# x loaded by features alone, its squares summed by TensorE, and a new order for the first stage of a diffusion block

## The chip, the cores and the metric

One core of one Trainium2 chip runs the whole kernel. The metric is device time in microseconds. One execution was also profiled; every time in the tables below is from that execution, unless it is called a median of the runs.

## What is computed

The reference is one layer of a hybrid block over 1024 tokens (a grid of 16 rows and 64 columns) of 1024 features, with 256 context tokens. Cut to what matters:

```python
def hybrid_layer(x, ctx, c, c_ctx, w_ada, b_ada, norm_g, w_in, ...):
    shift, scale, gate = adaln(c, w_ada, b_ada)           # silu(c) @ w_ada + b_ada
    shift_c, scale_c, gate_c = adaln(c_ctx, w_ada, b_ada)
    h = rmsnorm(x, norm_g) * (1 + scale) + shift          # mean of squares over the features
    hc = rmsnorm(ctx, norm_g) * (1 + scale_c) + shift_c
    q, k, v, za, u, bg, cg, zc = split(h @ w_in)          # 8 x 512 columns
    ...
    attn = neighbourhood_attention(q, k, v, kc, vc, rpb) * silu(za)
    conv = bg * conv3(cg * u) * silu(zc)
    return x + gate * (concat([attn, conv]) @ w_out)
```

All inputs and the output are float32.

## The kernel before, in words

Tokens lie in four blocks of 256. A float32 matrix product is made as three products of parts: each operand is split into a high part, rounded to the type that TensorE takes at full pace, and a low part, the rest (`hh` and `hl` for the normed x, `w[:, 0]` and `w[:, 1]` for a weight chunk). A step `fc` of one letter of these three is three products, one for each of three groups of 128 weight columns.

The stages follow one another: the first one (to about 64 us) makes the modulation, the normed x and the first three column groups; then come the q, k, v projections (the `pacc` products), attention with the gate projections as filler (`pu`), and the output product (`pout`).

The first stage is what the change touches. It is written as a list of words, `LOADS` and `STEPS` (lines 36 to 49), which `do` (line 750) reads one after the other; each word calls one helper through the table `does` (line 732). A number behind a word is a feature tile, k, of 128 features, or half and feature tile, or half, feature tile and which of the three products. While `strict` holds the engines (line 553), each engine and SyncE, which issues the loads, runs its instructions in exactly the order of the words. So an instruction that waits holds all that stand behind it on its engine. The words:

- `x`, `n`: rows of x or of the context, 128 tokens by 1024 features, 512 KB. `t` (half, k): x by features, 128 features by 512 tokens, 256 KB. `s` k: a slab of modulation weights, 1 MB, three buffers. `c` k, `q` k: a weight chunk of 128 by 384, 192 KB, five buffers, for the first column groups and for the first `pacc` tile. `e`: the context by features. `g`: gain tables.
- `sq` (line 584): ScalarE squares a row tile and sums it over the features by its accumulator. `root`: VectorE adds epsilon, GpSimd takes the power -1/2. `Rt` and `R` (line 595): TensorE spreads the 512 factors over all partitions, ScalarE copies them to SBUF.
- `T` (line 633): TensorE turns the first two feature tiles of half 0 out of the rows; `v` (line 637) multiplies these by the factors.
- `pr` (line 603): the modulation products of one slab, 32 narrow products. `tp`, `ab` (lines 611, 615): VectorE turns them and makes scale and shift of feature tile k.
- `u`, `hi`, `lo` (lines 623, 649, 655): VectorE scales a feature tile, ScalarE adds the shift and rounds to the high part, VectorE makes the low part. Scaling and low part are one VectorE instruction each, with both tensors in SBUF.
- `ch`, `cl` and `qh`, `ql` (lines 673, 678): a chunk's high part by ScalarE, its rest by VectorE. `rg` (line 699): VectorE multiplies rotation tables by gains, GpSimd prepares the gains.
- `fc` (line 665): the products of a feature tile with its chunk; product 0 is high by high, 1 takes the chunk's rest, 2 takes the low part of x.
- `warm`, `fill`: products of zeros that fill TensorE's waits. `conv`: steps of the gated convolution on the finished groups.

Behind the stage, line 1188 starts the first `pacc` tile (`proj_tile`, line 307), which reads the chunks' high parts and rests in the order of k. Much later, the loop over attention quarters (line 1321, n to 34) and line 1449 lead into the last stage; ScalarE's function there changes from Exp to Silu at the gates `zs` (line 500), which loads a table.

## Time and profile before

| | us |
|---|---|
| median of 3 runs | 590.03 (589.93 to 590.26) |
| profiled execution, its own time | 589.67 |
| its span | 587.8 |
| TensorE busy | 578.4 |
| VectorE busy | 438.9 |
| ScalarE busy | 282.2 |
| GpSimd busy | 57.4 |
| first `acc` product starts | 16.58 |
| first `pacc` product starts | 63.83 |

A profile row reads: start, duration, engine, line, operation, output <- inputs, shapes, count, and in brackets the idle time of the engine just before it and what ended that. PE is TensorE, DVE VectorE, ACT ScalarE, POOL GpSimd, SP SyncE. All instructions that go through the ordering helper carry line 71, so rows are told apart by their tiles. In a row of windows, the numbers behind each engine are its busy time and its count, then come the clock that TensorE was granted, the share of the DMA engines and GB/s. In a row of waits stand the total, the number of waits and the longest.

### The profile page before, as it was taken

Reading aid. Unit: us, or ns where it says so; the run is one execution under the profiler, and the core shown is the slowest. Engines: PE = TensorE matmul, PEld = TensorE weight load, DVE = VectorE, ACT = ScalarE, POOL = GpSimd, SP = SyncE. Lnnn points to the kernel's source line nnn. Section 1 sums busy time; section 2 is a strip of 40 time slices with the busy share of each in tenths; the row PEclk is TensorE's granted clock in tenths of the full one; section 3 lists DMA queues with packets and bytes.
Section 4 is the critical chain, followed back from the end, with each engine's and each line's share of the span. In section 5 each row is a group of like instructions: output and inputs, shape, how many; then the busy total and the mean of one; then the engine's idle time right before and its main releaser. Section 6 shows DMA issues by size and latency. Waiting matters only on the chain.

```text
span 587.8 us, 9905 instructions
## 1 busy us (share of the span) xinstructions
PE 578.4 (98%) x3532; PEld 483.4 (82%) x3532; DVE 438.9 (75%) x890; ACT 282.2 (48%) x652; POOL 57.4 (10%) x82
## 2 busy tenths in 40 slices
PE   8899999999999999999999999999999999999997
PEld 4578899999999999988878787878787866888886
DVE  1578779755846745367998788998978897999952
ACT  5636355436525546333463464466545646543420
POOL 1001024123123222100000000000000001100000
PEclk9999999999999999999999999999999999999999
DMA  8997576946765786685253647555757273673532
GB/s 327 410 413 268 177 258 188 308 149 219 247 207 186 249 302 233 213 314 200 92 191 129 241 139 224 195 209 160 251 188 254 93 251 114 231 249 88 200 125 90
DMA packets 66678, 126.14 MB, mean 215 GB/s; under 512 B 8713, under 2 KB 27649, under 8 KB 64324
## 3 DMA queue, kind: packets, MB, share of 16 engines
q1 hardware_dynamic: 66244, 124.70, 60.9%
q0 software_dynamic: 384, 0.81, 0.6%
q8 instruction: 28, 0.46, 0.3%
q14 instruction: 22, 0.18, 0.1%
HBM read 92.38 MB, written 33.10 MB: 213 GB/s over the span
## 4 chain that ended last, share of the span: by engine, by line
PE 89%; DMA 4%; DVE 3%; ACT 2%; issue 1%; SPq 0%; POOL 0%; DVEq 0%; ACTq 0%
PE pu L71 29%; PE pacc L71 22%; PE pout L71 13%; PE acc L71 5%; PE po L71 4%; PE cacc L71 4%; PE pss L71 3%; DMA xn<-in_xb 3%; PE pc L71 3%; PE pmx L71 2%; PE trA L71 1%; PE tr L71 1%; DMA y_d<-tb 1%; PE trB L71 1%; ACT sqj L71 1%
## 5 line engine op out<-in xcount | busy, mean ns | idle before, releaser
L71 PE MATMUL pu<-h,uh 128*128 128x512 f32 x544 | 174.6, 402 | 0.5 <-ACT zs L71 0.5
L71 PE MATMUL pacc<-w,h 128*128 128x384 f32 x768 | 138.9, 337 | 1.1 <-ACT ub L71 0.6
L71 PEld LDWEIGHTS pacc<-w,h 128*128 128x128 f32 x768 | 132.7, 188 | 1.9 <-ACT ub L71 1.1
L71 PEld LDWEIGHTS pu<-h,uh 128*128 128x128 f32 x544 | 97.3, 188 | 19.3 <-issue 1.2
L71 PE MATMUL pu<-h,ul 128*128 128x512 f32 x272 | 106.5, 392 | 0.0
L71 PE MATMUL pout<-right,left 128*128 128x512 f32 (+2 forms) x348 | 77.0, 383 | 0.0
L71 PEld LDWEIGHTS pout<-right,left 128*128 128x128 f32 x348 | 64.4, 188 | 12.7
L71 PEld LDWEIGHTS pu<-h,ul 128*128 128x128 f32 x272 | 51.1, 188 | 11.5
L71 POOL TENSOR_TENSOR ss<-ss,few 128x4 f32<-128x4 f32 (+1 forms) x40 | 41.4, 1035 | 126.7 <-DVE ss L71 126.4
L71 ACT COPY sc<-pc 128x512 f32<-128x512 f32 x32 | 18.7, 587 | 44.8 <-PE pc L71 44.8
L71 ACT ACTIVATE sc<-sc 128x512 f32<-128x512 f32 x32 | 20.3, 633 | 34.3 <-DVE sc L71 34.1
L71 PE MATMUL acc<-h,w 128*128 128x512 f32 x144 | 35.3, 397 | 1.4 <-ACT h L71 1.4
L71 ACT ACTIVATE sq<-pacc 128x256 f32<-128x256 f32 x32 | 12.4, 387 | 47.0 <-PE pacc L71 46.3
L71 DVE TENSOR_TENSOR sum<-sum,sb 128x372 f32<-128x372 f32 (+2 forms) x64 | 31.1, 486 | 2.8
L71 DVE SCALAR_TENSOR_TENSOR m<-pout,ab,m 128x512 f32<-128x512 f32 (+2 forms) x34 | 22.9, 717 | 13.2 <-PE pout L71 13.1
L71 PEld LDWEIGHTS acc<-h,w 128*128 128x128 f32 x144 | 26.3, 188 | 7.8 <-ACT h L71 2.1
L71 ACT ACTIVATE qn<-pacc,ss 128x64 f32<-128x64 f32 x128 | 30.0, 330 | 4.9 <-PE trA L71 2.5
L71 DVE TENSOR_TENSOR mx<-mx,sb 128x372 f32<-128x372 f32 (+2 forms) x64 | 30.8, 482 | 1.4
L71 DVE TENSOR_REDUCE ss<-sq 128x4 f32<-128x260 f32 (+1 forms) x40 | 15.7, 393 | 21.6 <-ACT sq L71 21.5
L71 DVE TENSOR_TENSOR ul<-uraw,uh 128x512 fp32r<-128x512 f32 x34 | 23.1, 686 | 9.4 <-ACT uh L71 9.4
L71 DVE TENSOR_TENSOR sb<-pss,bt 128x192 f32<-128x192 f32 (+3 forms) x48 | 27.6, 602 | 2.5 <-PE pss L71 2.5
L71 DVE TENSOR_TENSOR sb<-sb,mg 128x744 f32<-128x744 f32 (+2 forms) x32 | 26.6, 833 | 0.0
(142 smaller groups left out, 848.6 us busy)
## 6 DMA issues: line engine op xcount, KB each, us to landing
uraw<-in_w_col SPq DMA_DIRECT2D x34, 256.0 KB, 4.2
slab<-in_w_mod SPq DMA_DIRECT2D x8, 1024.0 KB, 8.9
q_d<-qs SPq DMA_DIRECT2D x32, 256.0 KB, 4.3
k_s<-k_d SPq DMA_DIRECT2D x8, 1024.0 KB, 7.3
q_s<-q_d SPq DMA_DIRECT2D x16, 512.0 KB, 3.7
wr<-in_w_grp SPq DMA_DIRECT2D x40, 192.0 KB, 5.0
bt<-in_rpb SPq DMA_DIRECT2D x8, 564.0 KB, 7.2
xn<-in_xb SPq DMA_DIRECT2D x8, 512.0 KB
```

Source lines behind the costliest of these rows:

```text
L71: i = emit(*a, **kw)
```

## The change

x is no longer loaded by rows. All 16 tiles by features are loaded, those of half 0 first, into the place that later holds feature tiles 6 and 7 of the normed x. The sums of squares are made from them: ScalarE squares the even and VectorE the odd feature tiles (`xs`), TensorE multiplies each by ones, in four groups of 128 tokens, which add up over the features in one bank (`xp`), ScalarE copies the bank (`cp`), TensorE turns the four rows into columns (`sl`), VectorE adds epsilon out of that bank (`root`, now `shifted`), and GpSimd takes the power as a word of its own (`po`). The first scaled tile reads the spread factors from PSUM.

All rests of chunks but the first, and the gain tables, are made by GpSimd and not by VectorE. The shift of a feature tile is made by ScalarE (`sh`). The small vectors come turned from the host, so TensorE and VectorE no longer turn them. The order of all words is new: half 1 follows half 0 by several feature tiles, the three products of a tile need not come together, and `done` counts them to mark the first and last of a bank. An activation of Silu on one element is put behind the last attention quarter.

```diff
-LOADS = "x0 x1 x2 x3 s0 c0 s1 c1 x4 x5 x6 x7 t10 t11 s2 t02 t12 c2"
+LOADS = "t00 t01 t02 t03 i0 t04 t05 t06 t07 s0 c0 s1 c1 s2 c2"
 STEPS = [
...
+    "ch7 rg0 u12 fc061 hi11 tp7 qh0 lo06 fc101 sh7 ab7 hi12 lo11 u07 u13 qh2 fc060 fc100 hi13 lo12 u14 fc102",
...
-    vec = bmp.tile([P, 3 * 384], F32, name="vec", tag="bt", bufs=2)[:, :P]
-    sp.dma_start(vec[:nvec], vecs)
-    sp.dma_start(ci, cst[:, 0:P])
+    sp.dma_start(vecT, vecs)
...
+    def feature_square(half, k):
+
+        squares[half, k] = xp.tile([P, 512], F32, name="sqf", tag="sqf", bufs=3)
+        if k % 2:
+            dve.scalar_tensor_tensor(squares[half, k], xh[half, k], 1.0 / D, xh[half, k], ALU.mult, ALU.mult)
+        else:
+            act.activation(squares[half, k], xh[half, k], AF.Square, scale=1.0 / 32)
+
+    def stat_bank(half):
+        return acc0[2 * half][1]
+
+    def feature_sum(half, k):
+
+        v = squares.pop((half, k))
+        for g in range(4):
+            pe.matmul(stat_bank(half)[32 * g:32 * g + 32, :P], onef, v[:, g * P:(g + 1) * P],
+                      start=taken[half] == 0, stop=taken[half] == KT - 1, skip_group_check=True)
+        taken[half] += 1
+
+    def sums_copy(half):
+        tokens[half] = xp.tile([P, P], F32, name="tk", tag="tk", bufs=1)
+        act.copy(tokens[half], stat_bank(half)[:, :P])
+
+    def sums_turned(half):
+        pe.matmul(stat_bank(half)[:, 256:260], tokens[half], ident[:, 0:P:32], start=True, stop=True)
...
-        dve.tensor_scalar(a[:, 0], rows[k][:, 0:2], bsh[:, k:k + 1], None, ALU.add)
+
+    def shift(k):
+        a = ab[:, k].rearrange("p (w j) -> p j w", w=2)
+        act.activation(a[:, 0], rows[k][:, 0:2], AF.Identity, bias=bsh[:, k:k + 1])
...
-        dve.tensor_tensor(v, early(k), spread_r[0], ALU.mult)
+        dve.tensor_tensor(v, xh[0, k], turns[0] if k == 0 else spread_r[0], ALU.mult)
...
-        dve.tensor_tensor(w[:, 1], raw, w[:, 0].bitcast(F32), ALU.subtract)
+        (dve if raws is chunks and k == 0 else pool).tensor_tensor(w[:, 1], raw, w[:, 0].bitcast(F32), ALU.subtract)
...
-        dve.tensor_tensor(tables[1][:, n, :, k], rraw, gqk[:, k:k + 1].broadcast_to([P, NB, HD]), ALU.mult)
+        pool.tensor_tensor(tables[1][:, n, :, k], rraw, gqk[:, k:k + 1].broadcast_to([P, NB, HD]), ALU.mult)
...
             quarter(n)
+            if n == 34:
+                act.activation(few[:, 5:6], ones, AF.Silu)
```

GpSimd's order in the first stage, before (`sums` is the power of the sums of squares, `rw` and `gkc` prepare the gains, `ss` belongs to the `pacc` tiles of the next stage):

```order
L71 TENSOR_TENSOR sums_161<-sums_161,few 128x4
L71 TENSOR_TENSOR sums_162<-sums_162,few 128x4
L71 TENSOR_TENSOR sums_163<-sums_163,few 128x2
L71 TENSOR_SCALAR rw_707<-rw_707 128x64
L71 TENSOR_TENSOR gkc<-rw_707 128x64
L71 MEMSET cu 128x1 x2
```

And the same place now (`w` are the rests of chunks, `cl` and `ql`; `rg` the gain tables):

```order
L72 TENSOR_TENSOR sums_159<-sums_159,few 128x4
L72 TENSOR_TENSOR w<-wr,w 128x384 x5
L72 TENSOR_TENSOR sums_160<-sums_160,few 128x4
L72 TENSOR_TENSOR w<-wr,w 128x384
L72 TENSOR_SCALAR rw_640<-rw_640 128x64
L72 TENSOR_TENSOR gkc<-rw_640 128x64
L72 TENSOR_TENSOR rg<-rw_640 128x8x64
L72 TENSOR_TENSOR w<-wr,w 128x384 x3
L72 TENSOR_TENSOR rg<-rw_640 128x8x64
L72 TENSOR_TENSOR w<-wr,w 128x384 x4
L72 MEMSET cu 128x1 x2
L72 TENSOR_TENSOR rg<-rw_640 128x8x64
```

Fifteen subtractions and four table products have come in between; behind the last row shown stand the third power, the fourth `rg` and the last two subtractions.

ScalarE's order at the end of attention, before (`ptot` and `po` are the last head's sums and output, `zs` the gates of the last unit):

```order
L71 ACTIVATE cv<-cu,vecT 128x512
L71 COPY sums<-ptot 128x256
L71 COPY ob<-po 128x512
L71 CAST uh<-uraw 128x512
L71 ACT_TABLE_LOAD
L71 ACTIVATE zs<-pu 128x512 x2
```

And now:

```order
L72 ACTIVATE cv<-cu,vecT 128x512
L72 ACT_TABLE_LOAD
L72 ACTIVATE few<-oner 128x1
L72 COPY sums<-ptot 128x256
L72 COPY ob<-po 128x512
L72 CAST uh<-uraw 128x512
L72 ACTIVATE zs<-pu 128x512 x2
```

The table load has moved ahead of three instructions, to behind the last convolution tap.

## The prediction

> **What bounds the kernel now.** I read the page first, then the list of who waited for whom on TensorE, then TensorE's own timeline of the first 80 us, then the other engines there. The page and the waits:

> ```profile
> PE 578.4 (98%) x3532; PEld 483.4 (82%) x3532; DVE 438.9 (75%) x890; ACT 282.2 (48%) x652; POOL 57.4 (10%) x82
> PE acc L71 <- ACT h L71: 1.4, 3, 0.6
> PE tr L71 <- DMA slab<-in_w_mod: 0.7, 1, 0.7
> PE pacc L71 <- ACT ub L71: 0.6, 1, 0.6
> PE pu L71 <- ACT zs L71: 0.5, 1, 0.5
> PE pacc L71 <- DVE w L71: 0.4, 1, 0.4
> ```

> TensorE is busy 98% of the span, so what an edit is worth is the time by which TensorE's work moves. All the waits together are a few us, nearly all in the first stage. That stage ends where the first `pacc` product starts:

> ```profile
> 16.58 2.34 PE L71 MATMUL acc<-h,w 128*128 128x512 f32 x9 [0.60 <-ACT h L71]
> 25.55 1.10 PE L71 MATMUL tr<-slab,c 128*32 128x64 f32 x64 [0.65 <-DMA slab<-in_w_mod]
> 31.79 5.08 PE L71 MATMUL acc<-h,w 128*128 128x512 f32 x21
> 36.79 1.10 PE L71 MATMUL tr<-slab,c 128*32 128x64 f32 x64
> 37.83 5.05 PE L71 MATMUL acc<-h,w 128*128 128x512 f32 x21
> 58.17 5.02 PE L71 MATMUL acc<-h,w 128*128 128x512 f32 x21
> 63.83 4.11 PE L71 MATMUL pacc<-w,h 128*128 128x384 f32 x22 [0.64 <-ACT ub L71]
> 68.37 8.94 PE L71 MATMUL pacc<-w,h 128*128 128x384 f32 x50 [0.42 <-DVE w L71]
> ```

> 21 `acc` products take 36.79 - 31.79 = 5.00 us, 0.238 each, so a step `fc` (three) is 0.714; one slab's products take 37.83 - 36.79 = 1.04. From 27 us on TensorE never rests for long: **the end of the stage is TensorE's own sum**, and the stage's loss lies ahead of 27 us. Its last waits put `pacc`'s steady run at 63.83 + 0.42 = 64.25, the number to compare with below.

> **The change, part by part.**

> *x by features alone.* Four MB of token rows are no longer loaded. What is then left ahead of a slab decides when its products can run. The third slab had 8.4 MB issued ahead of and with it (0.1 of constants, 4.2 of rows, 0.5 of columns, three slabs of 1.05, two chunks of 0.2) and landed at 25.5 (its row above). Under load the stage moves 0.41 MB a us:

> ```profile
> 20.00:30.00 10.00, 8.40 (x97) 5.39 (x95) 4.50 (x10) 5.17 (x10) 1.02 (x1) 1.00 1.03 410
> slab<-in_w_mod SPq DMA_DIRECT2D x8, 1024.0 KB, 8.9
> 9.41 1.06 ACT L71 ACTIVATE sqj<-xn 128x1024 bf16<-128x1024 f32 x1
> ```

> Now eight slabs, all of x's columns (4.2) and seven chunks are 14.1 MB, so the last slab lands at 25.5 + (14.1 - 8.4)/0.41 = 39.3. That was the bound to be removed: before, it landed near 39.9 (its issue) + 8.9 = 48.8, beside dense TensorE work. The queue is not starved by its buffers: the last slab waits for the fifth slab's products, which come about 10 us earlier.

> *The start.* As many bytes lead x's first half as before (2.1 MB), whose last tile is there at 9.4 (row above). From there: two squares queued on ScalarE to 10.8, the last sums 11.9, copy and turn 12.6, VectorE's add 12.8, the power on GpSimd 1.03 to 13.9, four transposes 14.6, the scaled tile after the chunk's rest 15.8, the high half 16.7. TensorE has seven fillers and the second slab's products ahead of the first `fc`, to 17.2. So the first product comes 0.6 later than 16.58; I take that, between 1 earlier and 1.5 later. What is gained is what follows.

> *TensorE's sum.* From 17.2: 48 `fc` of 0.714 (34.3), six slab products (6.2), eight feature sums (32 records of 64 columns are 0.52, so 8 of 128 are 0.26 each: 2.1), transposes 0.7, three fillers 0.6: 43.9, to 61.1 if dense. By the other road: the last slab's products run at about 39.9 to 41.0, and 30 `fc` stand behind them: 21.4, to 62.4. I take 62.4: against 63.2 (58.17 + 5.02) a gain of 0.8. The `ub` wait of 0.64 goes too, since half 0's groups now end earlier and its copy with them.

> *The subtractions that went to GpSimd.* 15 `cl`/`ql` of 384 columns and four `rg` of 512 leave VectorE. GpSimd had no such shape; its nearest rows, and VectorE's beside them:

> ```profile
> L71 POOL TENSOR_TENSOR kn<-kn,gkc x8: 480/500/909, 94.2 to 217.9; 128x128 f32<-128x128 f32 x8
> L71 POOL TENSOR_TENSOR gkc<-rw 128x64 f32<-128x64 f32 x1 | 0.3, 324 | 0.4 <-DMA rw<-in_k_norm_g 0.4
> ```
> ```profile
> 92.30 1.92 POOL L71 TENSOR_TENSOR ss<-ss,few 128x4 f32<-128x4 f32 x1 [2.75 <-DVE ss L71]
> 94.20 1.54 POOL L71 TENSOR_TENSOR kn<-kn,gkc 128x128 f32<-128x128 f32 x2
> 217.47 0.95 POOL L71 TENSOR_TENSOR kn<-kn,gkc 128x128 f32<-128x128 f32 x2
> 10.91 1.03 POOL L71 TENSOR_TENSOR sums<-sums,few 128x4 f32<-128x4 f32 x1 [9.14 <-DVE sums L71]
> ```
> ```profile
> 92.14 0.55 DVE L71 TENSOR_TENSOR w<-wr,w 128x384 fp32r<-128x384 f32 x1
> 92.60 0.42 DVE L71 TENSOR_TENSOR rot<-qn,rope 128x256 f32<-128x256 f32 x1
> 92.94 0.42 DVE L71 TENSOR_TENSOR rtmp<-qn,rope 128x256 f32<-128x256 f32 x1
> 93.39 0.49 DVE L71 TENSOR_TENSOR rot<-rot,rtmp 128x128 f32<-128x128 f32 x2
> 93.81 1.61 DVE L71 SCALAR_TENSOR_TENSOR gacc<-gs,c,gacc 128x512 f32<-128x512 f32 x2
> 217.67 0.91 DVE L71 TENSOR_TENSOR rot<-rot,rtmp 128x128 f32<-128x128 f32 x2
> 30.89 1.41 DVE L71 SCALAR_TENSOR_TENSOR h<-hw,ab,h 128x512 fp32r<-128x512 f32 x2
> ```

> 64 columns take 0.324 and 128 take 0.48: in a straight line 384 take 1.10 and 512 1.42 (bounds for 384: 0.48, and three times the slowest `kn`, 2.7). These rows show more: **the two engines hold each other up**. Two `rot` sums take 0.49 alone, and 0.91 beside two `kn`: 0.21 lost per `kn`. Two `kn` take 0.95, and 1.54 beside two `gacc` sums, whose operands also both lie in SBUF. By columns, VectorE loses 3 x 0.21 = 0.63 per subtraction, 0.84 per `rg` (bounds: nothing, and the whole 1.10).

> [...]

> Does it reach TensorE? After the last slab VectorE's chain starts with half 1's spread scale, about 39.7. Ahead of `u15` stand 15 steps of 1.41/2 = 0.705 (10.6), the last rows' 0.5 and about 0.9 of waits for ScalarE: 51.7. `fc151`, 20 steps behind the last products, is due at 41.0 + 20 x 0.714 = 55.3; with ScalarE's 0.9 for `hi15` that leaves 2.7 of cover. In the same stretch GpSimd runs five subtractions, the gain products and two `rg`: 5 x 0.63 + 0.2 + 2 x 0.84 = 5.0 lost. **5.0 - 2.7 = 2.3 late**, so the `fc` end at 64.7 (between 62.4 and 67).

> GpSimd's own queue: behind the gain tables, near 41.8, it has nine subtractions (9.9), four `rg` (5.7), the gain products (0.8) and a power (1.0): 17.4, half a VectorE step of waiting for each (4.5), and waits for ScalarE's casts of some 3: 66.7. `Rt2` waits for that power (three instructions earlier), and the third `wl` of the first `pacc` tile, chunk 3, is last of all: `pacc` reads it 1.9 after its start, 64.8 + 1.9, against about 67.4 with its release. I take 0.7 more (bounds 0 and 3).

> *Squares, `sh`, vecs.* Eight squares on each of two engines are 0.6 to 0.75 each; the second half's lie beside TensorE's wait for slabs. The turned vecs drop one transpose and a copy early on, hidden by the loads.

> *Silu's table.* It is loaded while ScalarE waits:

> ```profile
> 489.68 0.82 ACT L71 ACTIVATE cv<-cu,vecT 128x512 f32<-128x512 f32 x1
> 493.50 0.37 ACT L71 COPY sums<-ptot 128x256 f32<-128x256 f32 x1 [3.00 <-issue]
> 494.90 1.28 ACT L71 ACT_TABLE_LOAD   x1
> 496.19 1.09 ACT L71 ACTIVATE zs<-pu 128x512 f32<-128x512 f32 x2
> 496.84 0.73 PE L71 MATMUL pu<-h,uh 128*128 128x512 f32 x2 [0.51 <-ACT zs L71]
> ```

> 1.28 moves into an idle 3.0, `zs` comes 1.28 earlier, and TensorE's 0.51 goes.

> **The sum.** `pacc` runs steadily from 64.7 + 0.1 + 0.7 = 65.5 instead of 64.25: +1.25. Less 0.5 at the end: +0.75, say +0.9 with half of the start's skew. TensorE is dense behind it, so nothing gives that back. The profiled execution took 589.67 (span 587.8), the median of the runs is 590.03; I add to the median: **590.9 us**, on its own between 589.6 and 593.

> **Rivals.**
> - *The cover holds* (VectorE loses little, say 0.2 per subtraction): TensorE's sum alone counts. 62.5 against 64.25, and 0.5 at the end, is -2.2; with a start 0.3 later than I have it, 588.1. For it: `gacc`'s two took 1.61 against 1.41 for such a pair, only 0.1 per `kn`. Against it: `rot`.
> - *GpSimd is starved*, the slow side: if it gets its turn only where VectorE pauses, its queue falls behind, and `Rt2` and chunk 3 decide. At 92.30 a power on four columns took 1.92 instead of 1.03, through a subtraction and two products of VectorE, till the pause before 93.39. 0.9 on each of the last five instructions ahead of the last `wl` is 4.5 more than VectorE's loss: about 594.5. It decides once GpSimd's end passes 67. [...] `kn` at 94.20, which came between the two `gacc`, speaks against.
> - *The gains cancel* (about 0.4 lost per subtraction): 589.7.
> - *A cold start* adds to any of them. Six fillers took 2.74 at first, 14 then 3.79:

> ```profile
> 1.52 2.74 PE L71 MATMUL acc<-warm 128*128 128x512 bf16 x6 [1.52 <-POOL warm L71]
> 4.48 3.79 PE L71 MATMUL acc<-warm 128*128 128x512 bf16 x14
> ```

> 0.46 against 0.27 each. With nine fillers instead of 20 and gaps while x lands, the first `fc` could run at the slow pace: five of them would cost 5 x 0.5 = 2, some hidden under later waits.

> **Chances.** Forecast 0.52, cover holds 0.24, cancel 0.10, starved 0.14 (cold start spread over them). About 0.2%, 1.2 us, is what a measurement here can tell from no change: 588.85 to 591.2. The forecast's own range lies 0.24 in it and 0.28 above. Faster 0.24; same 0.24 + 0.10 = 0.34; slower 0.28 + 0.14 = 0.42. The range runs from the cover case with a start 0.4 earlier, 587.7, to the starved case, 594.2.

> **What would show it.** Right: `w` on GpSimd of 1.0 to 1.8 us, VectorE's two-operand steps at 0.9 to 1.5 beside them, TensorE waiting for `h` between 45 and 60 us, then for GpSimd's `w` in the first `pacc` tile; first `fc` near 17.2, last slab near 39; no wait on `zs`. Wrong: a dense TensorE from 41 us (then the cover case), the first `fc` before 16, a last slab after 42, or `pacc` waiting for anything but GpSimd.

## The result, and the profile after

The changed kernel takes 594.19 us (median of 4 runs, 593.36 to 595.78) against 590.06 for the kernel before: ratio 1.0073 (95% interval 1.005 to 1.0095), 4.1 us slower where 0.9 was forecast, at the upper end of the range. The profiled execution took 593.74 (span 591.9).

Who waited for whom on TensorE, in the changed kernel (total, times, longest, us):

```profile
PE tr L72 <- issue: 3.5, 2, 2.3
PE acc L72 <- ACT sqf L72: 2.4, 3, 1.5
PE acc L72 <- DVE sqf L72: 1.2, 1, 1.2
PE acc L72 <- DVE h L72: 0.6, 1, 0.6
```

The waits for `zs`, `ub` and `w` are gone, and so is the slab's. The largest is one that the prediction did not foresee: 3.5 us in which TensorE, in the middle of slab products (`tr`), waited for nothing that the trace shows. Its timeline:

```profile
15.28 0.65 PE L72 MATMUL tr<-ci,sums 128*128 128x128 f32 x4
17.37 1.08 PE L72 MATMUL tr<-slab,c 128*32 128x64 f32 x58
19.60 0.31 PE L72 MATMUL tr<-slab,c 128*32 128x64 f32 x6 [1.15 <-issue]
19.84 2.33 PE L72 MATMUL acc<-h,w 128*128 128x512 f32 x9
37.20 0.96 PE L72 MATMUL acc<-h,w 128*128 128x512 f32 x3
38.10 0.43 PE L72 MATMUL acc<-sqf,onef 128*32 128x128 f32 x8
38.45 0.96 PE L72 MATMUL acc<-h,w 128*128 128x512 f32 x3
43.86 0.99 PE L72 MATMUL tr<-slab,c 128*32 128x64 f32 x56
47.18 0.32 PE L72 MATMUL tr<-slab,c 128*32 128x64 f32 x8 [2.32 <-issue]
47.42 5.06 PE L72 MATMUL acc<-h,w 128*128 128x512 f32 x21
53.07 16.15 PE L72 MATMUL acc<-h,w 128*128 128x512 f32 x69 [0.58 <-DVE h L72]
69.19 12.75 PE L72 MATMUL pacc<-w,h 128*128 128x384 f32 x72
```

The first `fc` starts at 19.84 (forecast 17.2), the steady `pacc` at 69.19 (forecast 65.5, before 64.25). Both slabs' products break off after 58 and 56 of their 64 records. Behind 53 us TensorE is dense. A single `fc` between two feature sums takes 0.90 (37.20 to 38.10) and not 0.714.

VectorE behind half 1's factors, and GpSimd's groups in the first 72 us (busy time, mean ns of one):

```profile
43.66 1.88 DVE L72 SCALAR_TENSOR_TENSOR hw<-xh,ab,rs 128x512 f32<-128x512 f32 x2 [0.20 <-ACT rs L72]
45.67 1.83 DVE L72 SCALAR_TENSOR_TENSOR h<-hw,ab,h 128x512 fp32r<-128x512 f32 x1
47.53 1.39 DVE L72 SCALAR_TENSOR_TENSOR hw<-xh,ab,rs 128x512 f32<-128x512 f32 x1
49.01 1.33 DVE L72 SCALAR_TENSOR_TENSOR h<-hw,ab,h 128x512 fp32r<-128x512 f32 x1
50.27 0.97 DVE L72 TENSOR_SCALAR ab<-rw,b,vecT 128x2 f32<-128x2 f32 x1
51.16 1.85 DVE L72 SCALAR_TENSOR_TENSOR h<-hw,ab,h 128x512 fp32r<-128x512 f32 x1
57.15 2.93 DVE L72 SCALAR_TENSOR_TENSOR h<-hw,ab,h 128x512 fp32r<-128x512 f32 x2
```
```profile
L72 POOL TENSOR_TENSOR w<-wr,w 128x384 fp32r<-128x384 f32 x15 | 18.0, 1213 | 26.2 <-ACT w L72 26.2
L72 POOL TENSOR_TENSOR rg<-rw 128x512 f32<-128x512 f32 x4 | 5.1, 1279 | 0.0
```

GpSimd's subtraction takes 1.21 on average (1.10 forecast). Steps of VectorE that took 0.71 before take up to 1.85; the last `h` ahead of 53.07 is the low part that TensorE waits for there.

### The profile page after: what moved, and what is told of

The parts are those of the page before. It is cut to its first block, busy times and chain, and to the rows that moved or that the text cites. A ratio compares the mean times of both kernels' runs of the same rounds, so it can differ in the third digit from the quotient of the medians.

```text
span 591.9 us, 10108 instructions
## 1 busy us (share of the span) xinstructions
PE 578.6 (98%) x3638; PEld 483.7 (82%) x3638; DVE 443.7 (75%) x870; ACT 280.2 (47%) x655; POOL 80.8 (14%) x101
## 4 chain that ended last, share of the span: by engine, by line
PE 91%; DVE 4%; DMA 2%; ACT 1%; issue 1%; SPq 0%; DVEq 0%; ACTq 0%
PE pu L72 29%; PE pacc L72 23%; PE pout L72 13%; PE acc L72 6%; PE po L72 5%; PE cacc L72 4%; PE pss L72 3%; PE pc L72 3%; PE pmx L72 2%; PE tr L72 1%; PE trA L72 1%; DMA x<-in_xt 1%; DVE h L72 1%; DMA y_d<-tb 1%; PE ptot L72 1%; PE trB L72 1%
## 5 line engine op out<-in xcount | busy, mean ns | idle before, releaser
L72 ACT COPY sc<-pc 128x512 f32<-128x512 f32 x32 | 18.7, 588 | 45.4 <-PE pc L72 45.4
L72 DVE SCALAR_TENSOR_TENSOR m<-pout,ab,m 128x512 f32<-128x512 f32 (+2 forms) x34 | 22.9, 717 | 12.8 <-PE pout L72 12.7
L72 DVE TENSOR_REDUCE ss<-sq 128x4 f32<-128x260 f32 (+1 forms) x40 | 15.7, 393 | 21.6 <-ACT sq L72 21.5
L72 DVE TENSOR_TENSOR qs<-trA,qs 128x512 fp32r<-128x512 f32 x16 | 11.1, 692 | 21.2 <-ACT qs L72 20.3
## 6 DMA issues: line engine op xcount, KB each, us to landing
slab<-in_w_mod SPq DMA_DIRECT2D x8, 1024.0 KB, 8.2
k_s<-k_d SPq DMA_DIRECT2D x8, 1024.0 KB, 8.2
```

The source lines that it names most:

```text
L72: i = emit(*a, **kw)
```

## Experiments

Two theories. **Port**: while GpSimd reads, VectorE's steps with both tensors in SBUF are held up, as the two `rot` sums were beside two `kn` in the kernel before (0.91 instead of 0.49), and VectorE's late low parts move TensorE. "Port" and "lock" are names for this hold-up and no more; the traces show how long a step takes, not what it waits for. **Issue**, the rival: the feature sums add 256 small instructions to TensorE (eight products and as many weight loads for each of 16 tiles), its instructions come too late, and it stands still. Besides these: the start, the Silu, the place of the gain tables. All runs are below, each timed beside the kernel before on the same chip (its medians there were 589.54 to 590.06). The two columns of starts are of one profiled execution of each kernel, and that can lie more than a microsecond from the kernel's median: 589.21 for 588.13 in a_both, 591.00 for 591.98 in a_port, 594.97 for 593.31 in a_dve.

| | us | ratio to before (95%) | first `fc` | steady `pacc` |
|---|---|---|---|---|
| before | 590.06 | | 16.58 | 64.25 |
| changed | 594.19 | 1.0073 (1.0050 to 1.0095) | 19.84 | 69.19 |
| b_silu | 588.90 | 0.9988 (0.9979 to 0.9996) | 17.07 | 64.31 |
| a_mem | 591.68 | 1.0038 (1.0022 to 1.0055) | 19.83 | 66.43 |
| a_dve | 593.31 | 1.0066 (1.0052 to 1.0079) | 20.52 | 70.36 |
| a_wide | 592.52 | 1.0048 (1.0035 to 1.0061) | 18.64 | 67.34 |
| a_both | 588.13 | 0.9974 (0.9964 to 0.9984) | 19.11 | 64.21 |
| w_psum | 590.01 | 1.0001 (0.9992 to 1.0010) | 18.85 | 65.91 |
| w_start | 591.89 | 1.0032 (1.0019 to 1.0044) | 18.29 | 67.25 |
| w_all | 588.98 | 0.9986 (0.9977 to 0.9995) | 18.16 | 65.33 |
| w_many | 593.77 | 1.0076 (1.0061 to 1.0091) | 20.58 | 70.38 |
| w_clock | 592.01 | 1.0044 (1.0031 to 1.0058) | 19.28 | 67.97 |
| a_psum | 592.01 | 1.0044 (1.0031 to 1.0056) | 19.59 | 67.47 |
| w_best | 587.53 | 0.9964 (0.9952 to 0.9976) | 17.43 | 63.12 |
| a_order | 592.36 | 1.0048 (1.0034 to 1.0063) | 19.55 | 66.91 |
| a_port | 591.98 | 1.0036 (1.0024 to 1.0048) | 19.27 | 66.48 |
| w_order | 588.45 | 0.9986 (0.9975 to 0.9998) | 18.37 | 63.57 |

**b_silu: the Silu alone.** The kernel before, and

```diff
             quarter(n)
+            if n == 34:
+                act.activation(few[:, 5:6], ones, AF.Silu)
```

> The kernel before with nothing but the one-element Silu behind the last attention quarter. Of the change's parts this is the only one outside the first stage. All theories: TensorE's wait for zs (0.5 us) goes and nothing else moves, 589.5 against 590.06; if the table load were hidden anyway, 590.0.

588.90, 0.7 us less (0.0012 of 590; 0.2 to 1.2 by the interval). The wait for `zs` is gone and `pacc` starts where it did: the forecast's 0.5 holds. The first stage alone therefore lost some 4.8.

**a_mem: GpSimd fills with zeros in place of its subtractions and table products.** The changed kernel, and

```diff
-        (dve if ... k == 0 else pool).tensor_tensor(w[:, 1], raw, w[:, 0].bitcast(F32), ALU.subtract)
+        pool.memset(w[:, 1].bitcast(F32), 0.0)    # but chunk 0's
-        pool.tensor_tensor(tables[1][:, n, :, k], rraw, gqk..., ALU.mult)
+        pool.memset(tables[1][:, n, :, k], 0.0)
```

> The changed kernel, in which GpSimd's fifteen rests of chunks and four gain tables are replaced by fills with zero of the same tiles, so it reads nothing there and is done sooner; the output lacks these rests and tables. Port theory (GpSimd's reads hold up VectorE, which is what delays TensorE): VectorE's two-operand steps fall from 0.9 to 1.15 us back to 0.7 to 0.75, TensorE no longer waits for h at 53 us, pacc runs steadily from about 66.5 instead of 69.2, 591.5. Issue theory (TensorE's stall of 2.3 us for no wait that the trace shows, ahead of the last-but-one slab's end at 47 us, is as late by itself): the stall stays, pacc from about 68.5, 593.5. If the first feature sums and their single steps are what is lost, also 593 to 593.5.

591.68. The same VectorE steps in a_mem:

```profile
44.48 1.48 DVE L72 SCALAR_TENSOR_TENSOR hw<-xh,ab,rs 128x512 f32<-128x512 f32 x2 [0.18 <-ACT rs L72]
46.03 0.75 DVE L72 SCALAR_TENSOR_TENSOR h<-hw,ab,h 128x512 fp32r<-128x512 f32 x1
46.81 0.75 DVE L72 SCALAR_TENSOR_TENSOR hw<-xh,ab,rs 128x512 f32<-128x512 f32 x1
47.65 0.71 DVE L72 SCALAR_TENSOR_TENSOR h<-hw,ab,h 128x512 fp32r<-128x512 f32 x1
48.28 0.28 DVE L72 TENSOR_SCALAR ab<-rw,b,vecT 128x2 f32<-128x2 f32 x1
48.47 0.74 DVE L72 SCALAR_TENSOR_TENSOR h<-hw,ab,h 128x512 fp32r<-128x512 f32 x1
53.36 1.41 DVE L72 SCALAR_TENSOR_TENSOR h<-hw,ab,h 128x512 fp32r<-128x512 f32 x2
```

Row by row the changed kernel lost 0.40 + 1.08 + 0.64 + 0.62 + 0.69 + 1.11 = 4.5 ahead of 53 us, and 1.5 on the last pair. TensorE waits for no `h` here, and `pacc` comes 2.76 earlier. The port theory holds: GpSimd still writes in this stretch (seven fills from 45.36 to 48.15), and VectorE's steps are back at 0.75. My expectation that the late stall stays did not: the one at 17 to 20 us is there (0.98), another of 0.59 at 26, none at 45. So the 2.76 are the hold-up and the late stall together; the hold-up alone, with no such stall on either side, is a_wide against a_both below, 67.34 against 64.21.

**a_dve: the rests back on VectorE.** The changed kernel with `dve` for `pool` in the two lines above, nothing left out.

> The changed kernel with the fifteen rests and four gain tables on VectorE, as in the kernel before, in the new order of words; GpSimd keeps the powers and the gain products. Port theory: VectorE's other steps fall to 0.7, but it gets 15 x 0.55 and 4 x 0.6 us of its own back, 10.7 in all, of which some 4 us lie ahead of lo11 and u15; that is about what the lock cost there, so 593.5 to 595. If the order leaves VectorE no room, 596 to 598. If VectorE is not what decides, 594 as the changed kernel.

593.31, about the changed kernel; the intervals overlap. VectorE's other steps behind half 1's factors fall to 0.74 (`h`) and 0.755 (`hw`), as expected, and yet in this order it has not room enough for its own 10.7 us: TensorE waits 0.23, 0.79 and 0.49 behind the last slab's products. The profile holds a stretch at half clock (last section), so the place of `pacc` says little.

**a_wide: one product per feature.** The changed kernel, and

```diff
-        for g in range(4):
-            pe.matmul(stat_bank(half)[32 * g:32 * g + 32, :P], onef, v[:, g * P:(g + 1) * P], ...)
+        pe.matmul(stat_bank(half)[0:32], onesr, v, ...)      # v, onesr in the split type
...
-        pe.matmul(stat_bank(half)[:, 256:260], tokens[half], ident[:, 0:P:32], start=True, stop=True)
+        for g in range(4):
+            pe.transpose(stat_bank(half)[:, 32 * g:32 * g + 32], tokens[half][0:32, g * P:(g + 1) * P], ident[0:32, 0:32])
```

> The changed kernel with each feature's squares summed by one product of 512 columns in place of four products of 128 columns with a float32 operand: 2 instructions instead of 16 on TensorE per feature, its four sums then in one row and turned by four small transposes. Issue theory (the many small instructions empty TensorE's instruction fetch): the stalls without a cause at 17 to 20 and at 44 to 47 us go, pacc from about 67 to 68, 592 to 593. Port theory: the late stall goes too or not, but VectorE's lo11 still ends near 53, pacc from 68.5 to 69, 593.5 to 594.

592.52, `pacc` at 67.34. No stall without a cause is left anywhere in the first 80 us; the first `fc` comes 1.2 earlier, and a single `fc` between sums takes 0.70 (35.70 to 36.40 in its timeline). The sum of one feature, 512 columns in the split type, takes 0.23 (36.40 to 36.63), where the four float32 products of 128 took 0.35 (38.10 to 38.45 above). What is left are waits for VectorE and, behind it, ScalarE:

```profile
17.61 1.10 PE L72 MATMUL tr<-slab,c 128*32 128x64 f32 x64
18.64 2.33 PE L72 MATMUL acc<-h,w 128*128 128x512 f32 x9
43.03 5.10 PE L72 MATMUL acc<-h,w 128*128 128x512 f32 x21
49.39 3.04 PE L72 MATMUL acc<-h,w 128*128 128x512 f32 x12 [1.26 <-DVE h L72]
53.26 3.01 PE L72 MATMUL acc<-h,w 128*128 128x512 f32 x12 [0.84 <-ACT h L72]
56.83 10.54 PE L72 MATMUL acc<-h,w 128*128 128x512 f32 x45 [0.56 <-DVE h L72]
```

1.26 + 0.84 + 0.56 = 2.66. Both theories are true of a part.

**a_both: the two edits together.**

> The wide sums and the zero fills together: neither TensorE's fetch nor GpSimd's reads can cost. The output lacks the rests and tables that the fills replace. If the two causes are all that there is besides the start: TensorE dense from the last slab's products, 30 steps of 0.714 behind 43.0, pacc steadily from 64.6, 589.2. If a third thing waits behind them (ScalarE's casts, the last x tiles), pacc stays above 65.5, 590 or more.

588.13, 1.7 under the 589.86 of the kernel before beside it; `pacc` at 64.21, rather late, as this profile took 1.1 more than the median. TensorE runs 30 steps in one row:

```profile
43.52 20.71 PE L72 MATMUL acc<-h,w 128*128 128x512 f32 x90
```

By `pacc`, the edits bring 2.76 and 1.85 alone, 4.98 together; by the medians, each less that of the kernel before beside it, 2.2 and 1.4 alone, 5.9 together. Together they bring more than the sum, since each cause hides part of the other. These two causes are what the changed kernel loses against the kernel before; nothing third waits behind them.

**w_psum: half 1's factors out of PSUM.** a_wide, and

```diff
-        "u": ... scale((h, k), xh[h, k], spread_r[h][:], k, 0),
+        "u": ... scale((h, k), xh[h, k], turns[1] if h else spread_r[0][:], k, 0),
-        "R": lambda g: copies[g](),
+        "R": lambda g: g == 1 or copies[g](),
```

> The wide sums, and the scaled tiles of half 1 read the spread factors from the PSUM bank in which TensorE leaves them and not from a copy in SBUF (ScalarE's copy is dropped), so these eight VectorE steps have one tensor in SBUF and not two. Port theory as I gave it (what suffers is a step with both tensors in SBUF): hw of half 1 falls from 0.9 beside GpSimd to 0.7, the h steps stay at 1.1 to 1.2, TensorE's waits for h of 2.7 us in all behind 48 us halve, pacc from 66 instead of 67.3, 590.6. Rival (any VectorE step that takes something from SBUF waits for GpSimd's instruction): hw stays near 0.9 and the time at 592 to 592.5.

590.01, better than either theory had it. The group of half 1's scaled tiles in the first 70 us, in a_wide and then in w_psum:

```profile
L72 DVE SCALAR_TENSOR_TENSOR hw<-xh,ab,rs 128x512 f32<-128x512 f32 x8 | 7.4, 929 | 0.4 <-ACT rs L72 0.3
```
```profile
L72 DVE SCALAR_TENSOR_TENSOR hw<-xh,ab,tr 128x512 f32<-128x512 f32 x8 | 5.9, 744 | 0.2
L72 DVE SCALAR_TENSOR_TENSOR h<-hw,ab,h 128x512 fp32r<-128x512 f32 x14 | 15.2, 1092 | 2.0 <-ACT h L72 1.9
```

With one tensor in PSUM a step takes 0.744 with GpSimd at work beside it, as alone; `h`, with both tensors in SBUF, stays at 1.09. TensorE's waits for `h` fall from 2.66 to 0.40 + 0.85, about half.

**w_start: a shorter start.** a_wide, x's half 0 as four transfers of two feature tiles, `fill3` for `fill7`, and chunk 0's rest behind the first scaled tile:

```diff
-LOADS = "t00 t01 t02 t03 i0 t04 t05 t06 t07 s0 c0 ..."
+LOADS = "t00 t02 t04 t06 i0 s0 c0 ..."
+            sp.dma_start(early[k // 4][:, k % 4:k % 4 + 2], xt[k:k + 2, :, 0:512].rearrange("k p n -> p k n"))
```

> The wide sums, x's half 0 loaded as four transfers of two feature tiles in place of eight, the first scaled tile ahead of chunk 0's rest on VectorE, and three fillers of zeros in place of seven ahead of the second slab's products. Start theory (each issue on SyncE costs 0.46 us and the chain behind the last tile is what sets the first fc): last x tile about 1 us earlier, first fc at 17.0 to 17.5 instead of 18.64, and everything behind moves with it, pacc from 66.0, 590.6. Rival (the tiles come as fast as the memory gives them, or the later slabs hold TensorE back again): first fc not before 18.2, or pacc still above 67, 591.5 to 592.5.

591.89, `pacc` at 67.25 against 67.34: the rival holds. The last pair of tiles lands at 10.0 (issued at 2.67, 7.3 to landing; the seventh single tile of a_wide at 4.50 + 6.0 = 10.5), but the last sums of half 0 run at 12.19 (11.78 in a_wide), so fewer issues don't bring the sums earlier; the first `fc` gains 0.35, and it is spent by 32 us, where TensorE waits for `h` again.

**w_all: both together.**

> The edits of the two kernels before this one together, nothing left out. If start and port are separate terms they add: pacc from 64.7, 589.2, that is equal to or a little under the kernel before. If the slabs become the bound, pacc near 65.5, 590.

588.98, `pacc` at 65.33, 0.6 ahead of w_psum. The time is that of the first case, `pacc` nearer to the second, but TensorE waits for no slab.

**w_many: the small instructions alone.** a_wide with each filler of 512 columns as four of 128:

```diff
-            pe.matmul(ps, zeros if late else warm[:, :P], v, start=True, stop=True)
+            for a in range(4) if late else ():
+                pe.matmul(ps[:, a], zeros, zeros, start=True, stop=True)
...
```

> The wide sums, with each filler product of zeros (512 columns) split into four of 128 columns: the same columns, 120 instructions more on TensorE ahead of the first fc, about as many as the wide sums took away there. Issue theory: the stall without a cause near 18 us, gone with the wide sums, is back at 0.5 to 2 us, first fc at 19.2 to 20.5 instead of 18.64. If that stall came from the sums themselves (their float32 passes, their banks), no stall and first fc at 18.6 to 18.9.

The stall is back, in the same slab's products, though the sums are the wide ones and TensorE's columns are the same:

```profile
17.64 0.97 PE L72 MATMUL tr<-slab,c 128*32 128x64 f32 x52
20.23 0.42 PE L72 MATMUL tr<-slab,c 128*32 128x64 f32 x12 [1.62 <-issue]
53.08 17.33 PE L72 MATMUL acc<-h,w 128*128 128x512 f32 x69 [2.98 <-DVE h L72]
```

First `fc` at 20.58, 593.77. So the stall doesn't need the narrow sums themselves: it comes with the number of instructions, or with the place to which that number moves the packets of the instruction queue (last section). The run changes both and doesn't tell them apart. Its one wait for `h`, 2.98, also shows the hold-up's whole price where no second stall stands beside it (the wide kernel's 2.66 in three); its `pacc` is later still, because the clock is at half from 53 to 56 us (last section).

**w_clock: more fillers at the start.** a_wide with `warm13` for `warm9` and `fill10` for the first `fill6`.

> The wide sums with eight more fillers in TensorE's first two idle stretches (thirteen at the start, ten ahead of the fifth sum). Cold-start theory (what makes the runs scatter is a stretch of 3.4 us at half clock that follows TensorE's idle start): clocks of 0.997 in three of five runs with the wide sums become 0.999 or more in nearly all, median 591.9 instead of 592.5, runs within 1 us. Rival (the scatter comes from transfers and fetches): the same share of 0.997, 592.5.

592.01 against 592.52, intervals overlapping, and mean clocks of 0.996 or 0.997 in three of five runs as before: as far as five runs can tell, the idle start isn't what makes these runs scatter.

**a_psum: factors out of PSUM, alone.** w_psum's edit on the changed kernel.

> The changed kernel with one edit: half 1's scaled tiles read the spread factors from PSUM. Against the changed kernel's 594.2: VectorE's chain is 2 us shorter there, but the stall of TensorE at 45 us stays beside it. If the two hide each other: TensorE waits for h no more or less than 0.4, pacc from 68.4, 593.2 to 593.6. If the lock alone sets the end: 591.7 as with the wide sums' difference.

592.01, `pacc` at 67.47: as much as the wide sums, and the stall at 45 us is now 0.35. In the changed kernel the low part that TensorE needs ends at 53.01 whether TensorE stands still at 45 us or not (53.02 in w_many, without that stall): the hold-up set the end there, and the stall stood in its shadow. Why the stall is shorter here is open.

**w_best.** w_all, w_clock's fillers, and GpSimd's tables behind its rests:

```diff
-    "ch7 rg0 u12 ...  ... fc132 rg1 hi15 ...  ... rg2 fc172 po2 fc171 rg3 ql6",
-    "ql3 conv0 Rt2 R2 e0 e1 e2 e3",
+    "ch7 u12 ...  ... fc132 hi15 ...  ... fc172 po2 fc171 ql6",
+    "ql3 conv0 e0 e1 e2 e3 rg0 rg1 rg2 rg3 Rt2 R2",
```

> The wide sums, spread factors from PSUM, x in pairs, the eight more fillers, and GpSimd's gains and gain tables put behind all its rests (the context's columns issued ahead of them), nothing left out. If what is left of the port's cost comes from the two tables among the rests (1.0 us of waits for h behind 48 us): 588.2, as with the zero fills. If the rests alone do it: 589.0 as without this edit. If the rotation tables come too late for their first reader at 82 us: 590 or more.

587.53, 2.4 us under the kernel before (0.9952 to 0.9976), with nothing left out. From 42 us on TensorE waits for nothing in the stage:

```profile
42.19 20.96 PE L72 MATMUL acc<-h,w 128*128 128x512 f32 x90
63.12 12.75 PE L72 MATMUL pacc<-w,h 128*128 128x384 f32 x72
```

**a_order: the tables moved, alone**, on the changed kernel.

> The changed kernel with only GpSimd's gains and four gain tables put behind all its rests (the context's columns issued ahead of them). If VectorE's hold-up is as long as GpSimd works in the stretch behind half 1's factors, taking 3.9 us of GpSimd's work out of it shortens VectorE's chain to lo11 and u15 by 1.5 to 2.5 us: pacc from 67 to 67.8 where TensorE's stall at 45 us is short, 592 to 592.8. If the rests alone hold VectorE as much: 593.5 to 594.2.

592.36, `pacc` at 66.91, and no wait for `h` in the list: without the two tables and the gains among the rests VectorE is nearly in time. Something of the hold-up is left, since the 30 steps and the transposes take 21.2 (45.68 to 66.91), and 20.7 in a_port below. The stalls are 1.72 and 0.87 here.

**a_port: tables moved and factors from PSUM**, on the changed kernel.

> The changed kernel with that order and with half 1's factors read from PSUM; the sums stay in four products each, nothing is left out. Port theory whole: no wait for VectorE's h behind 46 us, the time that the zero fills gave, 591.2 to 591.8, and TensorE's stalls without a cause stay (1.5 to 3.5 us in all). If something of the hold-up is still there: a wait for h of 0.5 or more, 592 or more.

591.98, `pacc` at 66.48, that of the zero fills to 0.05. The time is 0.2 above the expectation. Its stalls without a cause, 1.15 + 0.37 + 0.63 = 2.15, are what it still has and w_order has not.

**w_order: without start and fillers.**

> The wide sums, the factors from PSUM and that order, without the paired loads, the changed start and the more fillers of the best kernel. If the order makes the difference of the best kernel to the one before it: 587.9 to 588.2, first fc at 18.6, TensorE dense behind 43 us. If the start makes it: 589.0.

588.45 and `pacc` at 63.57: order and PSUM factors bring the wide kernel 3.8 of `pacc`'s time, all but 0.45 of what w_best has. The rest goes with the first `fc` (18.37, 17.43); which of the start's edits that is, is open.

## Why the prediction was wrong

By its own steps, from 65.5 to the measured 69.19. The two steps that failed are the start and TensorE's sum: together they put the last slab's products at 43.86 instead of 39.9, 4.0 late. What follows took 0.3 less than forecast (25.3 from there to `pacc`, 25.6 forecast).

*The start* is two thirds of it. First `fc` at 19.84 and not 17.2, outside the bounds I gave (16.2 to 18.7). The spread transposes ended at 15.93 (15.28 + 0.65), 1.3 behind the 14.6 that I had. The x tiles are most of it; the seventh landed at 10.5 (issued at 4.50, 6.0 to landing), where I had all of them at 9.4, and ScalarE and VectorE could square the fifth and sixth only here:

```profile
9.27 0.63 ACT L72 ACTIVATE sqf<-x 128x512 f32<-128x512 f32 x1 [4.70 <-DMA x<-in_xt]
9.95 0.69 DVE L72 SCALAR_TENSOR_TENSOR sqf<-x 128x512 f32<-128x512 f32 x1 [2.15 <-DMA x<-in_xt]
```

Behind these ScalarE had two squares more and VectorE one, which ended at 12.25 (10.8 forecast) and had waited 0.91 for a square's buffer that TensorE's sums free. Most of the rest is the stall of 1.15, for which the sum had no term.

*TensorE's sum* is the other third. I had 22.7 from the first `fc` to the last slab's products: 21.5 of TensorE's own work, "if dense", and 1.2 in which it waits for the slab. Measured are 24.0 without any wait for a slab, so the work was 2.5 too small. A product at 0.238 was read from groups of 21; groups of nine took 2.27 from start to start and not 2.14, 0.5 in four of them (the prediction's own row at 16.58 has 2.34 for nine). Six singles took 5.1 instead of 4.3, eight sums 2.5 instead of 2.1, and 0.7 went in waits for a square and the power. So half 1's scaled tiles began at 43.66 (39.7 forecast), and all behind them came as much later.

a_wide shows what the narrow sums have in both steps: without them the first `fc` comes 1.20 earlier, and the stretch behind it takes 23.36 (18.64 to 42.00). That is 1.9 of the 4.0: I gave TensorE's instructions no cost, though the change adds 256 of them and I had written of their number only as columns. The other half, late x tiles and short groups, stays with the wide sums; in w_best the stretch is still 23.7 (17.43 to 41.16).

*The port*: right that GpSimd's reads hold VectorE up, and nearly in size. VectorE lost 4.5 ahead of the first low part that mattered and 1.5 behind it (5.0 forecast); TensorE paid 2.3 in the forecast, 2.66 in a_wide, 2.98 in w_many, and in the changed kernel 2.90, of which 2.32 read as the second stall and 0.58 as a wait for `h` (with less of the hold-up, in a_psum and a_order, the stall was shorter too, 0.35 and 0.87). The place was off: `lo11`, the second step of half 1, was late, not `u15`. "Two-operand steps" was too narrow: `ab`, 128x2 with scalars, went from 0.28 to 0.97. Not held up were VectorE's steps with one tensor in PSUM (0.744 in w_psum, with GpSimd at work beside them) and, behind half 1's factors, those beside GpSimd's fills (0.75 in a_mem); but at 15.85 in a_mem, beside fills, `ab` took 1.18. Why `ab` is held up is not shown.

*GpSimd's own queue*: wrong, and favourable. 0.7 was put down for chunk 3's rest; it was done at 70.49, 1.3 behind the start of `pacc`, and `pacc` ran 72 records without a wait. The starved case, which decided on the same rest, is refuted: GpSimd's subtraction took 1.21 and it was VectorE that waited.

*Last slab*: it landed at 42.2 (39.3 forecast; later than 42 was to be a sign of being wrong):

```profile
33.78 0.33 SPq L72 DMA_DIRECT2D slab<-in_w_mod  x1
slab<-in_w_mod SPq DMA_DIRECT2D x1, 1024.0 KB, 8.4
```

It was not waited for, but only because its products could not start before 43.86 anyway: one miss hid the other, and that is luck. It was late with the start: in w_best, with the first `fc` at 17.43, it landed at 39.5 (30.89 + 8.6), as forecast.

*`ub`, Silu*: right. `ub` was not waited for, and 0.5 became 0.7.

*Other rivals*: the cover did not hold (2.7 was allowed; at `lo11` there was 1.5: in a_mem that step ends at 49.2 and TensorE's seven steps from 45.72 at 50.7). A cold start was not in the profile: nine `fc` records took 2.33.

What each part was worth, by `pacc`'s time: hold-up 2.8 (69.19 to 66.43), narrow sums 2.2 to 2.9 more (66.43 to 64.21, 66.48 to 63.57); by the medians against the kernel before, 2.2 and 3.5 to 3.7. Without both, `pacc` starts up to 0.7 ahead of the kernel before, and with the Silu that is 1.1 (w_order) to 1.7 us (a_both).

## What to carry to other kernels

Count instructions as well as columns where a change swaps one wide product for many small ones: a stall on "issue" in the middle of a dense group is the sign (1.15 and 2.32 us here), and it can hide inside another wait until that one goes. Before handing two-tensor work to GpSimd, look at what VectorE must do in that stretch; moving one operand to PSUM took about half of the price away here (2.66 to 1.25 of waits), and with GpSimd's optional work a few us later as well nothing of it was left (w_order). A miss of a forecast need not be the term that was disputed: here the disputed one was right to 0.6 us, and the start and the sum taken for granted were off by four.

## What the runs showed of the hardware

```profile
q8 instruction: 1, 0.02, 24.9%
```

One packet of 16 KB (28 in the whole execution are 0.46 MB), 24.9% of 16 engines for 0.25 us, so 1.0 us long. Eight of the stalls on "issue" above ended 2.1 to 2.6 us after such a packet began: changed kernel 17.25 and 19.60, 44.75 and 47.18; a_order 16.75 and 19.31, 43.00 and 45.43; a_port 16.50, 23.50 and 43.00, and 19.03, 25.96 and 45.56; w_many 17.75 and 20.23 (starts of the 0.25 us windows that held them). The kernel before has the same once, a stall of 0.41 that ended at 31.55 behind a packet at 29.00 (26.0% of 16 engines for 0.25 us). That such a packet brings TensorE's next instructions is inferred from these times. Behind most packets stands no stall: the changed kernel has six in its first 60 us and two stalls, a_wide five and none, though one of them began at 24.50 in the middle of slab products (24.31 to 25.34). What must come together for a stall is not settled. Why the packet of 44.75 came 1.75 later than those of a_order and a_port is not settled.

**The clock of a run.** In a_dve's profile TensorE's clock fell about 1 us behind a stall:

```profile
20.28 0.31 PE L72 MATMUL tr<-slab,c 128*32 128x64 f32 x6 [1.89 <-issue]
20.52 3.52 PE L72 MATMUL acc<-h,w 128*128 128x512 f32 x9
```
```profile
20.00:30.00 10.00, 9.72 (x158) 7.41 (x158) 6.49 (x14) 2.83 (x6) 0.00 (x0) 0.83 0.90 328
```

Nine `fc` records took 3.52 instead of 2.33, and the granted clock was 0.83 in these 10 us: half for some 3.4 of them (10 x 0.17 / 0.5); it stands at 0.50 from 21.5 to 24.5. In w_many's profile it is 0.50 from 53 to 56 us, behind the wait of 2.98. A wait doesn't always bring it: the changed kernel's stalls of 1.15 and 2.32 were followed by 1.00. Mean clocks of 0.997 or less came in 24 of 55 runs of the ten kernels in which TensorE waited 0.98 us or more at once between 15 and 60 us, and in 3 of 57 runs of the six others. That fits the changed kernel's scatter of 2.4 us; that the waits cause it is an inference from these counts.
